# Operations of two tensors moved from GpSimd to VectorE, inverses built from blocks of 16, attention tiles spread anew

## The chip, the core and the metric

The kernel runs on one core of a Trainium2 chip. Its engines are TensorE (PE in the profile, with PEld for its weight loads), VectorE (DVE), ScalarE (ACT), GpSimd (POOL) and SyncE (SP), which issues nearly all DMAs. The metric is the device time of one execution in microseconds, as the median of several runs; lower is better.

## The reference, cut to what matters

The reference is two layers in fp32 on a sequence of 1024 positions and a width of 1024. Layer 0 mixes by an RWKV-7 recurrence (8 heads of 64) and by differential attention (4 heads); layer 1 mixes by a gated MLP over chunks of 128 positions. After each mixing comes a layer norm, a feed-forward block with a causal convolution of width 3, and another layer norm.

```
p   = x @ ab_w_in                                    # projections of both mixers
y_r = rwkv7_mix(p[..., :1792], ...)                  # state = state*w + (state@a) b^T + v k^T, per position
y_d = diff_attention(p[..., 1792:], ...)             # softmax(q1 k1) - lam * softmax(q2 k2), causal, then rms norm
x   = layer_norm(ALPHA*x + concat(y_r, y_d) @ ab_w_out)
ffn = (silu(conv3(x @ w_gate)) * (x @ w_val)) @ w_down   # width 2816
x   = layer_norm(ALPHA*x + ffn)
# layer 1: chunked_spatial_gating(x) @ c_w_out instead of the two mixers, then the same feed-forward
```

## The kernel before

Activations lie transposed: a tile is 128 features by 512 positions (half h of the sequence). Each dense product is done to nearly fp32 accuracy from fp32r operands: `split` makes `hi = copy(src)` on ACT and `lo = src - hi` on an engine with two-tensor operations, and `mm3` runs three 128x512 matmuls (lo·hi, hi·lo, hi·hi). So every weight and activation tile costs one ACT copy and one subtraction of two tensors ("a split" below). `split` (L125 to L128) does the subtraction on GpSimd unless an engine is given.

The program has five parts in time:

1. **Projections and RWKV, 0 to some 745 us.** The recurrence is cut into 8 units, four pairs of heads for each half of the sequence. A unit computes its vectors and masked 64x64 products, then inverts a unit triangular 64x64 matrix for each of its two heads and eight chunks, then runs a chain of small matmuls. The inverse takes 32x32 diagonal blocks: they are stored to DRAM and loaded so that one block lies on one partition (`N`, L938); 31 steps of forward substitution follow, each a multiplication and an addition on VectorE that need each other's result (L943, L945); the results go through DRAM again (`d<-X`, `D<-d`), four 32x32 transposes place them (L960, L967), and 16 and 16 small matmuls (L963, L972) make the lower left block. `weave` puts a slice of other work after every step of a chain: matmuls of later projections or of the output projection, and tiles of attention (a head is eight query tiles). A chain has 16 steps. The table `AT = 0, 0, 0, 9, 9, 9, 8, 0` says how many attention tiles are spread over the chain of each unit.
2. **Output projection and first layer norm**, to some 805 us.
3. **Feed-forward of layer 0**, to some 1430 us, as products of 2x2 blocks with sums of blocks (Strassen's form), so that sums (L312, L341) are formed on VectorE and split before PE uses them. First come 22 products with `A12`, then four early products with `A11`, then the loop over 22 feature tiles f: six products each, sums, convolution (L325, L327), gating, and stores of the gated tiles to DRAM. The splits of weights and of two of the four activation sums (`T2`, `T3`) are on GpSimd, as is one of the two gating multiplications (L332). In the down half of the block all splits are on VectorE already.
4. **Gated MLP of layer 1**, to some 1800 us; its weights' splits are on GpSimd (`B.weng`).
5. **Feed-forward of layer 1 and the last layer norm**, to the end.

The order on each engine is made by a list scheduler from priorities and a timeline of its own; PE instructions of the fill are pinned behind the last matmul of a chain step. Each engine executes its list in order.

Of the kernel before, what the change touches and what calls it, by code (L numbers as in the profile page):

```python
# [24 lines left out]
F32 = mybir.dt.float32  # L25
# [34 lines left out]
class Builder:  # L60
# [3 lines left out]
    def __init__(self, tc, ctx, a):  # L64
# [9 lines left out]
        self.onesD = c.tile([P, P], F32, name="onesD")  # L74
        nc.gpsimd.memset(self.onesD, 1.0 / D)
# [4 lines left out]
        self.weng = self.gs = None  # L80
# [44 lines left out]
    def split(self, src, hi, lo, eng=None):  # L125
        nc = self.nc
        nc.scalar.copy(hi, src)  # L127
        (eng or nc.gpsimd).tensor_tensor(out=lo, in0=src, in1=hi.bitcast(F32), op=ALU.subtract)  # L128

    def load_w(self, src, n=1024, extra=False):  # L130
# [11 lines left out]
        self.split(raw[:, :n], hi[:, :n], lo[:, :n], self.weng)  # L142
# [47 lines left out]
    def ln_stats(self, s, z):  # L190
# [9 lines left out]
        for d in range(KT):  # L200
# [26 lines left out]
    def ln_apply(self, s, z, rs, g, b, xhl, out):  # L227
# [3 lines left out]
        for d in range(KT):  # L231
# [23 lines left out]
    def ffn(self, layer, xa, xd, lng, lnb, out=None, xout=None):  # L255
# [32 lines left out]
        def operand(src, tiles, eng=None):  # L288
            hl = [tiles.pop(0) for _ in range(2)]
            self.split(src, *hl, eng)  # L290
# [6 lines left out]
        def load_up(f, todo):  # L297
# [8 lines left out]
            for n in todo:  # L306
# [6 lines left out]
                W[f][n] = operand(src, wt, vec if n in WLO and len(todo) < 5 else pool)  # L313
                yield

        def load_p2(f):
            raw = raws()[:, :HW]
            sync.dma_start(raw, wup[f][:, HW:])
            W[f]["A12"] = operand(raw, wt, pool)
# [11 lines left out]
        def store(f, h, c, v, eng=vec):  # L331
            eng.tensor_tensor(out=c, in0=c, in1=v, op=ALU.mult)  # L332
# [5 lines left out]
        def second(n, k, tiles):  # L338
# [3 lines left out]
            X[n].append(operand(o, tiles, vec if n in LOV else pool))  # L342
# [41 lines left out]
        for f in list(fs) + [None]:  # L384
# [10 lines left out]
            if old:  # L395
# [3 lines left out]
                store(g, 1, c1_, V_, pool)  # L399
# [47 lines left out]
        def make(n, i):  # L447
# [268 lines left out]
class Rwkv:  # L716
# [13 lines left out]
    def consts(self):  # L730
# [6 lines left out]
        self.mask = B.cload("cmask", [P, 3, C], pool=pool)  # L737
        self.rst = B.cload("rst", [P, P], a["rst"].broadcast_to([P, P]), pool=pool)
# [45 lines left out]
    def unit(self, h, p, xs, out):  # L784
# [141 lines left out]
        d1 = B.dram.tile([2, 2, NC, 32, 32], F32, name=B.uid("d1"))  # L926
        d2 = B.dram.tile([2, 2, NC, 32, 32], F32, name=B.uid("d2"))
# [341 lines left out]
AO = 0  # L1269
# [276 lines left out]
```

## Time and profile before

| | us |
|---|---|
| median of 3 runs | 2465.79 (2461.41 to 2466.0) |
| profiled execution | 2462.04 |
| its span | 2459.9 |
| PE busy, weight loads busy | 2339.2, 1887.6 |
| DVE, ACT, POOL busy | 1811.1, 1042.4, 875.2 |

The profiled execution's own time is its span and 2.1 us around it. "Busy" of PE counts each matmul from its start to its modelled end, and matmuls overlap in the pipe, so PE can be shown busy throughout and still have slack between short groups. Averages over the span say little here, because the parts above have different limits; the windows below are cut along the parts.

### The profile page before, as it was taken

How to read it: one execution, taken by the hardware profiler on the slowest of the kernel's cores; microseconds unless marked ns; L12 is line 12 of the kernel's file. 1: busy time of each engine (PE TensorE's matmuls, PEld its weight loads, DVE VectorE, ACT ScalarE, POOL GpSimd, SP SyncE). 2: the span in 40 equal slices, each digit the busy share in tenths (PEclk: the TensorE clock that was granted, in tenths of full speed). 3: DMA queues.
4: the chain of work that ended last, by engine and by line, in shares of the span. 5: the costliest groups of instructions: out<-in, count | busy, mean ns of one | idle time of the engine just before them, and what ended most of it. 6: DMA issues, size and time to landing. Idle time of an engine off the chain costs nothing. (4 is left out here: it accounts for less than half of the span.)

```text
span 2459.9 us, 34226 instructions
## 1 busy us (share of the span) xinstructions
PE 2339.2 (95%) x12058; PEld 1887.6 (77%) x12058; DVE 1811.1 (74%) x3308; ACT 1042.4 (42%) x1903; POOL 875.2 (36%) x770
## 2 busy tenths in 40 slices
PE   8999998888998989999999999999989999999996
PEld 6777777766776867888878878888877788887886
DVE  5766778899888757777689867345377777779875
ACT  4323455555554633333344435334353333334434
POOL 2001110110005756665600026557566666640003
PEclk9999998998999989999999999999999999999998
DMA  5322352332423644333485625234373333358441
GB/s 189 90 73 80 90 179 76 94 102 86 124 68 122 219 137 134 122 118 120 129 271 173 198 81 174 85 109 133 109 234 116 124 122 110 120 168 294 132 147 69
DMA packets 180508, 326.99 MB, mean 133 GB/s; under 512 B 44912, under 2 KB 58096, under 8 KB 180336
## 3 DMA queue, kind: packets, MB, share of 16 engines
q1 hardware_dynamic: 176112, 316.93, 40.5%
q10 hardware_dynamic: 4224, 7.87, 1.1%
q8 instruction: 95, 1.56, 0.3%
q14 instruction: 77, 0.63, 0.1%
HBM read 261.55 MB, written 63.18 MB: 132 GB/s over the span
## 5 line engine op out<-in xcount | busy, mean ns | idle before, releaser
L128 POOL TENSOR_TENSOR wlo<-wraw,whi 128x1024 fp32r<-128x1024 f32 x54 | 133.9, 2482 | 275.9 <-PE ch L150 168.1
L127 ACT CAST whi<-wraw 128x1024 fp32r<-128x1024 f32 (+1 forms) x166 | 153.8, 929 | 169.1 <-PE sc L150 45.8
L327 DVE SCALAR_TENSOR_TENSOR lx<-pr,cw,lx 128x512 f32<-128x512 f32 x176 | 182.6, 1038 | 4.2
L328 ACT ACTIVATE lx<-lx 128x512 f32<-128x512 f32 x88 | 55.7, 633 | 278.8 <-DVE lx L327 278.8
L148 PE MATMUL pj<-x,wlo 128*128 128x512 f32 x310 | 126.7, 409 | 9.8 <-DVE wlo L128 8.5
L149 PE MATMUL pj<-x,whi 128*128 128x512 f32 x303 | 121.6, 401 | 0.0
L150 PE MATMUL pj<-x,whi 128*128 128x512 f32 x303 | 120.7, 398 | 0.0
L325 DVE TENSOR_SCALAR lx<-pr,cw 128x512 f32<-128x512 f32 x88 | 78.5, 893 | 49.4 <-DMA gd<-lx 47.9
L332 POOL TENSOR_TENSOR lx<-lx,bv 128x512 f32<-128x512 f32 x44 | 69.5, 1579 | 78.4 <-ACT lx L328 73.9
L128 DVE TENSOR_TENSOR wlo<-wraw,whi 128x1024 fp32r<-128x1024 f32 x66 | 80.5, 1220 | 16.6 <-ACT whi L127 16.2
L148 PEld LDWEIGHTS pj<-x,wlo 128*128 128x128 f32 x310 | 59.7, 193 | 26.7 <-ACT x L127 7.3
L754 POOL COPY lastc<-pr 128x1 f32<-128x1 f32 x28 | 9.4, 334 | 187.2 <-ACT pr L752 187.2
L943 DVE TENSOR_TENSOR sub<-X,N 128x60 f32<-128x60 f32 (+24 forms) x248 | 51.6, 208 | 24.2 <-DMA N<-d 19.9
L202 POOL TENSOR_TENSOR sg<-sg,x 128x512 f32<-128x512 f32 x1 | 1.3, 1288 | 191.0 <-ACT x L199 191.0
L149 PEld LDWEIGHTS pj<-x,whi 128*128 128x128 f32 x303 | 58.5, 193 | 13.2 <-issue 1.4
L150 PEld LDWEIGHTS pj<-x,whi 128*128 128x128 f32 x303 | 58.2, 192 | 12.9 <-issue 0.4
L1224 ACT ACTIVATE ap<-ap,mx 128x128 f32<-128x128 f32 (+7 forms) x64 | 49.5, 773 | 43.1 <-DVE mx L1221 42.5
L1216 PE MATMUL sc<-x,x 128*128 128x512 f32 (+2 forms) x192 | 58.1, 407 | 7.8 <-DVE mx L1221 4.5
L128 POOL TENSOR_TENSOR whi<-wraw,whi 128x512 fp32r<-128x512 f32 x32 | 46.7, 1460 | 26.2 <-ACT whi L127 23.5
L128 POOL TENSOR_TENSOR wlo<-wraw,wlo 128x512 fp32r<-128x512 f32 x32 | 46.1, 1439 | 27.2 <-ACT wlo L127 27.0
L945 DVE TENSOR_TENSOR X<-X,sub 128x60 f32<-128x60 f32 (+24 forms) x248 | 51.6, 208 | 4.9
L148 PE MATMUL pq<-x,wlo 128*128 128x512 f32 x128 | 52.6, 411 | 2.7 <-DVE wlo L128 2.7
(1755 smaller groups left out, 8079.6 us busy)
## 6 DMA issues: line engine op xcount, KB each, us to landing
wraw<-in_w_up_dram SPq DMA_DIRECT2D x64, 512.0 KB, 4.1
wraw<-in_w_dq_dram SPq DMA_DIRECT2D x104, 256.0 KB, 3.5
gd<-lx SPq DMA_DIRECT2D x88, 256.0 KB, 2.3
KB<-in_w_up_dram SPq DMA_DIRECT2D x32, 512.0 KB, 3.5
wraw<-in_w_rwkv_dram SPq DMA_DIRECT2D x28, 512.0 KB, 3.7
KB<-in_w_dq_dram SPq DMA_DIRECT2D x50, 256.0 KB, 3.3
lx<-gd SPq DMA_DIRECT2D x48, 256.0 KB, 3.6
pr<-ge SPq DMA_DIRECT2D x44, 256.0 KB, 2.7
```

The source lines that it names most:

```text
L127: nc.scalar.copy(hi, src)
L128: (eng or nc.gpsimd).tensor_tensor(out=lo, in0=src, in1=hi.bitcast(F32), op=ALU.subtract)
L148: mm(ps, wl, xh, start=first, stop=False, **kw)
L149: mm(ps, wh, xl, start=False, stop=False, **kw)
L150: self.last = mm(ps, wh, xh, start=False, stop=last, **kw).ins
L325: vec.tensor_scalar(out=c, in0=G[:, 0:HW], scalar1=cw[:, f, 0:1], scalar2=cw[:, f, 3:4], op0=ALU.mult, op1=ALU.add)
L327: vec.scalar_tensor_tensor(out=c, in0=G[:, j:j + HW], scalar=cw[:, f, j:j + 1], in1=c, op0=ALU.mult, op1=ALU.add)
L328: act.activation(c, c, AF.Silu)
L332: eng.tensor_tensor(out=c, in0=c, in1=v, op=ALU.mult)
L943: dve.tensor_tensor(out=t, in0=X[:, 0:n, j:j + 1].broadcast_to([P, n, w]), in1=N[:, j:j + 1, j + 1:].broadcast_to([P, n, w]), op=ALU.mult)
L945: self.sub = dve.tensor_tensor(out=X[:, 0:n, j + 1:], in0=X[:, 0:n, j + 1:], in1=t, op=ALU.add)
L1216: nc.tensor.matmul(ps[:, :max(w, 256)], q, k[c][s][:, :max(w, 256)], start=i == 0, stop=i == 1)
```

## The change

1. `split`, `load_w`, `operand`, `store`, `ln_stats` and `ln_apply` lose their choice of engine: the subtraction of every split, the second sum of squares of a norm and both gating multiplications are VectorE operations. On GpSimd stay the subtraction and the scaling of three of eight tiles in the last norm (`PD`), four shifts, one masking product, the powers of small tiles (`rsqrt`), copies and memsets. GpSimd's list shrinks from 742 rows to 274.
2. The inverse starts from 16x16 diagonal blocks: 15 steps of substitution on a tile that holds 2 blocks in a partition's rows, with operands of 8 to 36 elements, where 31 steps had 16 to 76. Two levels of joining follow on PE in 32x32 tiles of the array: 32 matmuls (L968), a masked multiplication (L973), 32 and 16 matmuls (L974, L981), four additions into `XF` and two into `D0`, then 16 and 16 matmuls as before (L987, L994). The stores and loads through DRAM are 8, 2, 2 and 8 DMAs where there were 4, 4, 4 and 4.
3. A chain has 18 steps, `weave` divides by 18, and `AT` gives 10, 10, 10, 5 attention tiles to units 4 to 7.
4. `onesD` is one column, read with a stride of zero.

```diff
-    def split(self, src, hi, lo, eng=None):
+    def split(self, src, hi, lo):
         nc.scalar.copy(hi, src)
-        (eng or nc.gpsimd).tensor_tensor(out=lo, in0=src, in1=hi.bitcast(F32), op=ALU.subtract)
+        nc.vector.tensor_tensor(out=lo, in0=src, in1=hi.bitcast(F32), op=ALU.subtract)
...
-                (nc.vector if d in LNV else nc.gpsimd).tensor_tensor(out=hl[1], in0=z[d], in1=hl[0].bitcast(F32), op=ALU.subtract)
+                nc.vector.tensor_tensor(out=hl[1], in0=z[d], in1=hl[0].bitcast(F32), op=ALU.subtract)
...
-                W[f][n] = operand(src, wt, vec if n in WLO and len(todo) < 5 else pool)
+                W[f][n] = operand(src, wt)
...
-            X[n].append(operand(o, tiles, vec if n in LOV else pool))
+            X[n].append(operand(o, tiles))
...
-                store(g, 1, c1_, V_, pool)
+                store(g, 1, c1_, V_)
...
+        Q = 16
+        d1 = B.dram.tile([2, 4, NC, Q, Q], F32, name=B.uid("d1"))
+        d2 = B.dram.tile([2, 4, NC, Q, Q], F32, name=B.uid("d2"))
         for e in range(2):
-            for b in range(2):
-                rows = slice(64 * e + 32 * b, 64 * e + 32 * b + 32)
-                self.dq.dma_start(d1[e, b].rearrange("c s t -> s c t"), MA[rows, e, :, 32 * b:32 * b + 32])
-        I = 4 * NC
+            for b in range(4):
+                self.dq.dma_start(d1[e, b].rearrange("c s t -> s c t"),
+                                  MA[64 * e + Q * b:64 * e + Q * b + Q, e, :, Q * b:Q * b + Q])
+        I = 8 * NC
...
-        for j in range(31):
-            w, n = 31 - j, j // 4 + 1
+        for j in range(Q - 1):
+            w, n = Q - 1 - j, j // 2 + 1
...
+        dve.transpose(out=DT.rearrange("p c t -> p (c t)"), in_=D0.rearrange("p c t -> p (c t)"))
+        for c in range(NC):
+            for i, o in enumerate(R4):
+                B.last = nc.tensor.matmul(p1[o, 0, c], MA[o, i // 2, c, 32 * (i % 2):32 * (i % 2) + 32], DT[o, c], start=True,
+                                          stop=True, tile_position=(32 * i, 32 * i)).ins
+        yield
+        dve.tensor_tensor(out=T1, in0=p1[:, 0], in1=self.low[:, None, :].broadcast_to([P, NC, 32]), op=ALU.mult)
+        for c in range(NC):
+            for i, o in enumerate(R4):
+                B.last = nc.tensor.matmul(p1[o, 1, c], D0[o, c], T1[o, c], start=True, stop=True, tile_position=(32 * i, 32 * i)).ins
+        yield
         for lo, hi in H:
-            dve.transpose(out=XF[lo, :, 0:32], in_=D0[lo])
+            dve.tensor_tensor(out=XF[lo, :, 0:32], in0=p1[lo, 1], in1=DT[lo], op=ALU.add)
+        p0, p1 = p1, self.ps.tile([P, 2, NC, 32], F32, tag="ch", bufs=NBANK["ch"], name=B.uid("p1"))
+        for c in range(NC):
+            for i, o in ((1, R4[1]), (3, R4[3])):
+                B.last = nc.tensor.matmul(p1[o, 1, c], T1[o, c], D0[o, c], start=True, stop=True, tile_position=(32 * i, 32 * i)).ins
+        for lo, hi in H:
+            dve.tensor_tensor(out=XF[hi, :, 32:64], in0=p0[hi, 1], in1=DT[hi], op=ALU.add)
+            dve.tensor_tensor(out=D0[hi], in0=p1[hi, 1], in1=D0[hi], op=ALU.add)
...
-AT = 0, 0, 0, 9, 9, 9, 8, 0
+AT = 0, 0, 0, 10, 10, 10, 5, 0
...
-            for _ in range((j * na + AO) // 16 - ((j - 1) * na + AO) // 16):
+            for _ in range((j * na + AO) // 18 - ((j - 1) * na + AO) // 18):
...
-        weave(i, fill, (FC, max(total / 16, FR[i] if i < 6 else 0)), AT[i])
+        weave(i, fill, (FC, max(total / 18, FR[i] if i < 6 else 0)), AT[i])
```

**VectorE, the substitution of the last unit.** `X_6600` before and `X_6902` now are the tile of the unit's inverse; ap, mx, f are of the attention, y, bv, BK of other units. Before:

```order
L945 TENSOR_TENSOR X_6600<-X_6600,sub_6616 128x29
L1227 RECIPROCAL f_6422<-l_6393 128x1
L1051 TENSOR_TENSOR y_6514<-y_6514,bv_4644 128x512
L1221 ISA ap_6408,mx_6417<-sc_6414,zero,mx_6412 128x384
L1221 ISA mx_6417 128x1
L943 TENSOR_TENSOR sub_6619<-X_6600,N_6599 128x28
L1052 TENSOR_TENSOR y_6514<-y_6514,pl_6521 128x512
L886 TENSOR_TENSOR bv_6530<-v_5873,bs_6528 128x512
L990 COPY BK_5084<-pf_6820 64x512
L1221 ISA ap_6408,mx_6419<-sc_6414,amask,mx_6417 128x128
L1221 ISA mx_6419 128x1
L945 TENSOR_TENSOR X_6600<-X_6600,sub_6619 128x28
```

Now:

```order
L947 TENSOR_TENSOR sub_6910<-X_6902,N_6901 128x15
L1072 TENSOR_SCALAR y_6812<-y_6812,c_rvec 128x512
L949 TENSOR_TENSOR X_6902<-X_6902,sub_6910 128x15
L1073 TENSOR_TENSOR y_6812<-y_6812,bv_4792 128x512
L947 TENSOR_TENSOR sub_6913<-X_6902,N_6901 128x14
L1074 TENSOR_TENSOR y_6812<-y_6812,pl_6819 128x512
L949 TENSOR_TENSOR X_6902<-X_6902,sub_6913 128x14
L1243 ISA ap_5798,mx_5802<-sc_5799,zero 128x128
L1243 ISA mx_5802 128x1
L947 TENSOR_TENSOR sub_6916<-X_6902,N_6901 128x26
```

The 62 instructions of a unit's substitution, one after the other and each in need of the one before, are 30 with half the elements. Here they stood over 157 rows of VectorE's list, between attention and other units' work, and stand over 46.

**TensorE, where the chain of the last unit begins.** `p` is the bank in which the blocks are joined, av, sc, tr and ot are attention, wo is the output projection. Before, with the second group of 16 standing 27 rows after the first:

```order
L150 MATMUL wo_7196<-x_5838,whi_7192 128x512
L148 MATMUL wo_7286<-x_5808,wlo_7283 128x512
L1240 MATMUL av_7065<-x_5565,x_5568 128x128 x4
L963 MATMUL p_7547<-XT_7544,MB_5931 32x32 x16
L1216 MATMUL sc_7221<-x_5564,x_5556 128x256
L1216 MATMUL sc_7221<-x_5560,x_5556 128x256
```

Now, the first of four places:

```order
L148 MATMUL wo_7527<-x_6000,whi_7523 128x512
L1258 MATMUL tr_6464<-ident,ap_6439 128x128 x2
L1262 MATMUL av_6468<-x_5709,x_5712 128x128 x2
L968 MATMUL p_7788<-XN_7786,MB_6124 32x32 x32
L1262 MATMUL av_6468<-x_5709,x_5712 128x128 x2
L1262 MATMUL av_6468<-x_5710,x_5711 128x128 x2
L1238 MATMUL sc_6565<-x_5707,x_5700 128x512
```

and the last two of them, which answer to the two groups of before:

```order
L1238 MATMUL sc_6584<-x_5702,x_5698 128x512
L148 MATMUL wo_7619<-x_6012,whi_7615 128x512
L780 MATMUL pl_7733<-lx_2483,lw_7731 128x512
L987 MATMUL p_7890<-XT_7785,MB_6124 32x32 x16
L1262 MATMUL av_6535<-x_5709,x_5711 128x128 x4
L1262 MATMUL av_6535<-x_5710,x_5712 128x128 x3
L994 MATMUL p_7890<-T_7787,D_6908 32x32 x16
L1005 MATMUL pf_7964<-LT_6125,XT_7785 64x128
```

Between these stand the 48 of L974 and L981, alternating, 19 rows after the group of 32; each group of the chain waits for a VectorE or ScalarE result of the one before.

**VectorE, where the loop of the first feed-forward block begins.** Lines L341 (now L339) form the activation sums, L250 and L128 (now L248 and L126) are splits, L312 (now L310) forms weight sums, L394 (now L392) adds a product to the gate. Before:

```order
L341 TENSOR_TENSOR k_6714<-k_6714,aa_6710 128x512
L341 TENSOR_TENSOR BK_7543<-BK_7543,LT_7541 128x512
L250 TENSOR_TENSOR x_8230<-BK_7543,x_8229 128x512
L341 TENSOR_TENSOR BK_7543<-BK_7543,LT_7541 128x512
L128 TENSOR_TENSOR x_8216<-e_6712,x_8215 128x512
L128 TENSOR_TENSOR x_8218<-e_6713,x_8217 128x512
L128 TENSOR_TENSOR x_8220<-k_6714,x_8219 128x512
L312 TENSOR_TENSOR sg_6709<-wraw_8348 128x512
L312 TENSOR_TENSOR k_6714<-KB_8350,wraw_8348 128x512
L312 TENSOR_TENSOR e_6713<-sg_6709,KB_8350 128x512
L312 TENSOR_TENSOR aa_6710<-KB_8350,e_6713 128x512
```

Now:

```order
L339 TENSOR_TENSOR BK_7784<-BK_7784,LT_7782 128x512
L126 TENSOR_TENSOR Z_8670<-aa_6960,Z_8670 128x512
L126 TENSOR_TENSOR x_8548<-e_6963,x_8547 128x512
L339 TENSOR_TENSOR BK_7784<-BK_7784,LT_7782 128x512
L126 TENSOR_TENSOR Y_8673<-MB_7783,XT_8672 128x512
L126 TENSOR_TENSOR x_8550<-k_6964,x_8549 128x512
L392 TENSOR_TENSOR pr_6968<-pr_6968,pj_8255 128x512
L126 TENSOR_TENSOR dg_8675<-BK_7784,Y_8674 128x512
L310 TENSOR_TENSOR sg_6959<-wraw_8678 128x512
L126 TENSOR_TENSOR o_8677<-BK_7784,y_8676 128x512
L126 TENSOR_TENSOR wlo_8656<-wraw_8678,wlo_8656 128x512
L310 TENSOR_TENSOR k_6964<-KB_8680,wraw_8678 128x512
```

The splits that had a list of their own on GpSimd now stand in VectorE's list between the sums, and what waits there for a load or a PE result holds them up as well.

## Rows read from the trace of the kernel before

**Rows 1.** The page's head: span, and busy time of each engine.

```profile
span 2459.9 us, 34226 instructions
...
PE 2339.2 (95%) x12058; PEld 1887.6 (77%) x12058; DVE 1811.1 (74%) x3308; ACT 1042.4 (42%) x1903; POOL 875.2 (36%) x770
```

**Rows 2.** Busy time by stretch: stretch, length, engines' busy us, PE's granted clock, DMA.

```profile
60.00:380.00 320.00, 316.35 (x2161) 249.62 (x2160) 228.87 (x554) 122.64 (x213) 33.25 (x74) 0.98 0.36 105
380.00:740.00 360.00, 322.60 (x2441) 258.24 (x2441) 318.95 (x1042) 203.94 (x480) 32.91 (x60) 0.91 0.31 89
...
860.00:960.00 100.00, 87.17 (x349) 68.29 (x348) 63.56 (x74) 35.12 (x63) 57.45 (x50) 0.93 0.41 133
960.00:1200.00 240.00, 239.01 (x1032) 193.31 (x1031) 180.77 (x205) 81.71 (x145) 150.55 (x129) 1.00 0.38 123
1280.00:1400.00 120.00, 120.00 (x525) 98.75 (x524) 107.11 (x176) 55.15 (x96) 0.00 (x0) 0.99 0.61 201
1500.00:1780.00 280.00, 280.00 (x1296) 231.57 (x1295) 132.86 (x228) 106.61 (x151) 165.48 (x91) 1.00 0.35 113
...
1840.00:1950.00 110.00, 97.51 (x394) 75.73 (x393) 81.86 (x91) 35.79 (x64) 67.24 (x56) 0.95 0.38 124
```

**Rows 3.** The page's costliest groups: tiles and shapes, count, busy us, mean ns, idle before.

```profile
L128 POOL TENSOR_TENSOR wlo<-wraw,whi 128x1024 fp32r<-128x1024 f32 x54 | 133.9, 2482 | 275.9 <-PE ch L150 168.1
...
L128 DVE TENSOR_TENSOR wlo<-wraw,whi 128x1024 fp32r<-128x1024 f32 x66 | 80.5, 1220 | 16.6 <-ACT whi L127 16.2
...
L943 DVE TENSOR_TENSOR sub<-X,N 128x60 f32<-128x60 f32 (+24 forms) x248 | 51.6, 208 | 24.2 <-DMA N<-d 19.9
...
L945 DVE TENSOR_TENSOR X<-X,sub 128x60 f32<-128x60 f32 (+24 forms) x248 | 51.6, 208 | 4.9
```

**Rows 4.** VectorE's groups with shapes kept apart, whole span.

```profile
L943 DVE TENSOR_TENSOR sub<-X,N 128x60 f32<-128x60 f32 x24 | 5.2, 217 | 0.4
...
L943 DVE TENSOR_TENSOR sub<-X,N 128x28 f32<-128x28 f32 x16 | 3.0, 185 | 0.3
...
L877 DVE TENSOR_TENSOR MB<-pm,c_cmask 128x256 f32<-128x256 f32 x32 | 13.4, 419 | 13.6 <-PE pm L875 13.5
...
L960 DVE STREAM_TRANSPOSE XT<-D 32x256 f32<-32x256 f32 x16 | 6.9, 433 | 7.9 <-DMA D<-d 7.7
```

**Rows 5.** PE in order of time, last unit's first small group: start, us, records.

```profile
685.58 1.09 PE L963 MATMUL p<-XT,MB 32*32 32x32 f32 x32
```

**Rows 6.** The same view at 168 us: 64x64 matmuls on two tiles in turn.

```profile
168.65 1.01 PE L902 MATMUL pw<-Z,MB 64*64 64x64 f32 x27
```

**Rows 7.** GpSimd in order of time, before the first and the second feed-forward loop.

```profile
842.97 1.63 POOL L128 TENSOR_TENSOR Z<-MB,Z 128x512 fp32r<-128x512 f32 x1 [1.89 <-ACT Z L127]
...
856.50 1.74 POOL L128 TENSOR_TENSOR dg<-BK,Y 128x512 fp32r<-128x512 f32 x1
...
1810.16 1.75 POOL L250 TENSOR_TENSOR x<-MB,x 128x512 fp32r<-128x512 f32 x1
...
1832.33 1.73 POOL L128 TENSOR_TENSOR o<-BK,y 128x512 fp32r<-128x512 f32 x1
```

**Rows 8.** VectorE in order of time, before the second feed-forward loop.

```profile
1806.57 0.68 DVE L128 TENSOR_TENSOR MB<-sg,MB 128x512 fp32r<-128x512 f32 x1
1807.17 0.68 DVE L341 TENSOR_TENSOR cs<-cs,r 128x512 f32<-128x512 f32 x1
...
1815.80 1.79 DVE L341 TENSOR_TENSOR e<-e,sg 128x512 f32<-128x512 f32 x1
```

**Rows 9.** What PE waited for from 860 to 960 us: total, times, longest.

```profile
PE ch L148 <- ACT bv L403: 5.2, 1, 5.2
PE pj L148 <- DVE pr L394: 3.4, 1, 3.4
```

**Rows 10.** VectorE's groups in the first feed-forward loop, 960 to 1200 us.

```profile
L327 DVE SCALAR_TENSOR_TENSOR lx<-pr,cw,lx 128x512 f32<-128x512 f32 x58 | 65.6, 1131 | 1.5
L325 DVE TENSOR_SCALAR lx<-pr,cw 128x512 f32<-128x512 f32 x30 | 27.9, 929 | 12.2 <-DMA gd<-lx 11.6
```

**Rows 11.** Waits of the whole span, the one of the convolution.

```profile
DVE lx L325 <- DMA gd<-lx: 47.9, 24, 4.8
```

More of the change, by code (lines that the diff above doesn't have):

```diff
@@ L73, in __init__ @@
         c = self.const
-        self.onesD = c.tile([P, P], F32, name="onesD")
-        nc.gpsimd.memset(self.onesD, 1.0 / D)
+        ones = c.tile([P, 1], F32, name="onesD")
+        nc.gpsimd.memset(ones, 1.0 / D)
+        self.onesD = ones.broadcast_to([P, P])
         self.ident = c.tile([P, P], F32, name="ident")
@@ L286, in ffn, with operand @@
         ra, rbc = Ring(self.ln.tiles), Ring(self.up.tiles)
-        def operand(src, tiles, eng=None):
+        def operand(src, tiles):
             hl = [tiles.pop(0) for _ in range(2)]
-            self.split(src, *hl, eng)
+            self.split(src, *hl)
             return hl
@@ L737, in consts @@
         self.mask = B.cload("cmask", [P, 3, C], pool=pool)
+        self.low = B.cload("low", [P, 32], pool=pool)
         self.rst = B.cload("rst", [P, P], a["rst"].broadcast_to([P, P]), pool=pool)
@@ L945, in unit @@
             self.sub = dve.tensor_tensor(out=X[:, 0:n, j + 1:], in0=X[:, 0:n, j + 1:], in1=t, op=ALU.add)
-        for g in range(4):
-            self.dq.dma_start(d2.rearrange("e b c (m g) t -> g (e b c) m t", g=4)[g], X[I * g:I * g + I])
+        for g in range(2):
+            self.dq.dma_start(d2.rearrange("e b c (m g) t -> g (e b c) m t", g=2)[g], X[I * g:I * g + I])
         yield True
         XF = self.t("XT", 1, (P, NC, C))
-        D0 = self.t("D0", 1, (P, NC, 32))
-        T1 = self.t("XN", 1, (P, NC, 32))
+        DT = self.t("XN", 1, (P, NC, 32))
@@ L961, in unit @@
-        for e, (lo, hi) in enumerate(H):
-            for c in range(NC):
+            for b in range(4):
+                self.dq.dma_start(D0[64 * e + Q * b:64 * e + Q * b + Q, :, b % 2 * Q:b % 2 * Q + Q],
+                                  d2[e, b].rearrange("c s t -> s c t"))
+        dve.transpose(out=DT.rearrange("p c t -> p (c t)"), in_=D0.rearrange("p c t -> p (c t)"))
[3 more added lines that the diff above has]
+                                          stop=True, tile_position=(32 * i, 32 * i)).ins
@@ L963, in unit @@
+        for c in range(NC):
[4 more added lines that the diff above has]
+            dve.tensor_tensor(out=D0[hi], in0=p1[hi, 1], in1=D0[hi], op=ALU.add)
+        for c in range(NC):
+            for e, (lo, hi) in enumerate(H):
                 B.last = nc.tensor.matmul(p1[hi, 0, c], MA[lo, e, c, 32:64], XF[lo, c, 0:32], start=True, stop=True,
@@ L966, in unit @@
         for lo, hi in H:
-            dve.transpose(out=XF[hi, :, 32:64], in_=D0[hi])
-        for lo, hi in H:
             act.copy(T1[hi], p1[hi, 0])
-        for e, (lo, hi) in enumerate(H):
-            for c in range(NC):
+        for c in range(NC):
+            for e, (lo, hi) in enumerate(H):
                 B.last = nc.tensor.matmul(p1[hi, 1, c], D0[hi, c], T1[hi, c], start=True, stop=True,
@@ L1515, in layout @@
     a["cmask"] = np.stack([strict, incl, strict], 1)
+    a["low"] = (s[:, None] % 32 >= 16) & (np.arange(32) < 16)
     a["rst"] = (np.arange(128) % 64 != 0).astype(f32)[None]
```

45 lines of the change are left out of this document (20 added, 25 removed).

## The prediction

> **What bounds the kernel now.** I first read the page's head and the busy time by engine: PE is busy 2339 of 2460 us [rows 1], so at most 121 us are open to any change that leaves the matmuls as they are. Then the windows by stretch, to see where these 121 us lie [rows 2]. The projections with the first units (60 to 380) leave 3.7 us of 320, the first feed-forward loop (960 to 1200) 1.0 of 240, the gated MLP (1500 to 1780) none. Two kinds of stretch leave much: the units with attention (380 to 740), 37.4 us of 360, and the entries of the two feed-forward loops, 12.8 of 100 and 12.5 of 110. Next the groups of the page and VectorE's groups by form, for the price of one instruction [rows 3, 4], and the engines in order of time at the places where the change acts [rows 5 to 8]; last the waits, for what PE lacks at a loop's entry [rows 9] and what VectorE lacks in the loop [rows 10, 11].
>
> The profiled execution took 2462.0 us, 2.1 of them outside its span, and 3.8 less than the median of the runs. The sum is made against 2462.0; since the profiled time lies low in a spread of 4.6 us, I add half of the 3.8 at the end. This kernel's measurement can't tell a difference under 0.2%, 4.9 us.
>
> **Term 1, substitution in units 5 to 8.** In 380 to 740 VectorE is busy 319 of 360 us, 89%, and PE idles 37 at a clock of 0.91: VectorE bounds here. A unit's substitution now is 31 steps of two instructions at 208 ns [rows 3], 62 x 0.208 = 12.9 us (L943 and L945 alike). Afterwards 15 steps of two, with a mean of some 25 elements. The forms give 185 ns at 28 elements and 217 at 60 [rows 4], 1 ns an element, so 182 ns: 30 x 0.182 = 5.5 us, 7.4 less. Of four transposes at 433 ns one stays: 1.3 less. New are seven VectorE operations (the masked product L973, four additions into XF, two into D0); the nearest row, a 256-wide one that reads PSUM, takes 419 ns [rows 4]: 2.9 more. Net 5.8 us a unit, 23 for four units. If PE follows VectorE fully, the stretch shrinks by 23/0.89 = 26; if the length is set by the chain's hops between engines, by nothing; all of PE's idle time is 37. I take 20, since the list of VectorE holds fewer rows between a chain's ends (46 where 157 stood) and VectorE was the fuller engine, but not fully busy. The attention is 35 tiles as before, and where they stand is within this term's range: with 10, 10, 10, 5 the last chain keeps five tiles beside it, where PE had filler from the output projection anyway.
>
> **Term 2, the joining on PE in units 1 to 4.** Small matmuls of a unit rise from 32 to 112 in the program's words, which are 64 and 224 records, since 32 records stand in half of a group. In 60 to 380 PE is full, so each costs. A group of 32 records on 32x32 tiles took 1.09 us [rows 5], 0.032 us each with the last one's tail of some 0.1 off; 27 of 64x64 on two tiles took 1.01 [rows 6], some 0.030 each with a last one's length of about 0.2 off. Before: 64 x 0.032 = 2.0 us. After: the 128 records of L968, L974 and L981 that go round all four row groups of the array I price at half, 0.016, as two pairs can run side by side; the other 96 at 0.030: 2.0 + 2.9 = 4.9 us, 2.9 more a unit. Bounds: all at 0.016 gives 1.5 more, all at 0.032 gives 5.1. For four units 12 us, 6 to 20. Units 5 to 8 pay the same 12 inside PE's idle 37 us: nothing; if term 1 took all of that idle time they would show too, which is why term 1 stands at 20 and not 37.
>
> The Trainium skill, "TensorEngine Tiling (Array Packing)", section "Instruction Overhead", gives every matmul an overhead of about 60 cycles, however narrow it is; by an estimate from it the 160 further records of a unit cost 25 ns each at full clock, 16 us for four units, and the sum would be 4 us higher. It lies close to the row's 0.030 and speaks against the half price above, though a group that rotates over four row groups is not in this trace.
>
> **Term 3, the entries of the two loops.** There the trace shows VectorE and GpSimd in lockstep. VectorE operations on 128x512 that meet no GpSimd work start 0.60 us apart and take 0.68; beside GpSimd's they take 1.79 [rows 8], as long as GpSimd's own, 1.75. GpSimd's 14 operations from 1810.16 to 1832.33 start 22.17 / 13 = 1.70 us apart [rows 7], and VectorE's with them. So a pair (one here, one there) costs 1.70, and two on VectorE alone 2 x 0.60 = 1.20. Before the second loop that gives 14 x 0.5 = 7 us. Before the first, 9 such operations stand from 842.97 to 856.50: 4.5. The first weight operands have five splits, which would go from some 1.3 to 0.6 each; counted half, since sums stand between them, 3.5 for both loops. Together 15. PE's waits there are for ScalarE and VectorE results, 5.2 and 3.4 us [rows 9], which both hang on these sums and splits. Bounds: 0, if the loads or ScalarE's copies are what is late, and 25, all that PE idles at the entries.
>
> **Terms at nothing, with their cover.** Loops in their steady part: in 240 us 129 GpSimd operations go to VectorE at 0.60, 77 us onto 181. What came from the lockstep goes: L327 has 58 at 1131 ns and L325 30 at 929 [rows 10]; at 0.60 they give back 31 and 10. So at most 217 of 240 us, less as the weight sums that met GpSimd also shorten. PE waits for nothing there, and VectorE stays below PE: 0. The cover is the 23 us or more that are left, and operands made ahead; the second rival is the case where it is gone. Gated MLP: 54 splits of 2.48 us on GpSimd become 1.22 on VectorE [rows 3], 66 us, and the other 37 operations 22, on 133: 221 of 280, under a PE that never waits: 0. The down halves have no GpSimd work already (1280 to 1400), so nothing changes. First layer norm, 780 to 800: its second sum of squares and splits leave GpSimd, 2 us less, an estimate between 0 and 4 from the same 0.5 per pair. The broadcast column, and 20 DMA issues a unit on SyncE where there were 16: no wait of PE rests on either, 0.
>
> **Sum.** 2462.0 - 20 + 12 - 15 - 2 = 2437, and half of 3.8 on it: 2439 us. The terms' bounds reach further than they are likely to go together; as the likeliest case's own range I take 2425 to 2455.
>
> **Rivals.**
>
> *The chain doesn't shorten.* A unit's chain now passes two more joins, each a PE group, an evacuation and a further group, and 8 DMAs where 4 stood before the substitution; VectorE's loads of N already cost 19.9 us of waits [rows 3]. If these hops take back what the 32 fewer instructions give, term 1 is 0: 2439 + 20 = 2459. For it: PE idles 37 us at 89% of VectorE, so it isn't VectorE alone. Against: weave puts filler between steps, and 18 steps hold as much as 16.
>
> *Matmuls quicken without GpSimd.* In the loop a 128x512 product takes 240/1032 = 232.6 ns, where GpSimd is idle (1280 to 1400) 120/525 = 228.6. If that is GpSimd's reading, two loops of 22 x 72 matmuls gain 3168 x 0.004 = 12.7 us, and with the small matmuls at their low price of 6 the time is 2439 - 13 - 6 = 2420. Against: in the gated MLP, where GpSimd is busiest (165 of 280), 280/1296 = 216 ns, though with narrower ones among them.
>
> *Slower: VectorE's one list.* In the loop the convolution's first operation waits for a buffer that a store has to leave (gd<-lx): 47.9 us in 24 waits [rows 11], 11.6 in these 240 us [rows 10]. Until now the weight splits ran on meanwhile in GpSimd's list; now they stand behind that wait. If half of it reaches PE, it costs 24 us, and the entries, where the same list decides, lose their 15: 2439 + 24 + 15 = 2478. With the entries' gain kept it decides from 23 us of PE idle in the loops upwards. For it: VectorE at up to 217 of 240 with waits of 12 a stretch is nearly full. Against: the wait is idle time that exists because VectorE was early, and a fuller VectorE comes later and finds the store done.
>
> **How the numbers follow.** The forecast 0.50, the quick matmuls 0.17, the unshortened chain 0.14, the one list 0.15, and 0.04 for nothing that counts. The range of 8 in 10 takes in the forecast, most of the quick matmuls, all of the unshortened chain and the low end of the slower case: 2408 to 2468. Faster by over 0.2% (under 2461): 0.49 of the forecast, 0.17, and 0.08 of the unshortened chain, 0.74. Within 0.2%: the rest of that chain's case 0.05, and 0.04 for the last, 0.09. Slower: 0.17, the one list with the tails.
>
> **What would show it.** Term 1: 30 substitution instructions a unit near 182 ns, and the stretch from 380 to the output projection some 20 us shorter at VectorE's share of about 89%; wrong, if PE's idle time there stays near 37. Term 2: four joins a unit with 64 records at about 1.0 us (L968) and PE in the first units some 3 us a unit longer; the low bound shows as 0.016 a record in all. Term 3: VectorE's 128x512 operations 0.60 apart at the entries, GpSimd near 100 us in all, and PE's idle time there 10 and 8 us smaller; wrong, if PE then waits for loads. Terms at nothing: PE idle in 240 us of a loop still 1 to 2 us; if it is over 8, the slower rival runs. The prediction is wrong as a whole if the loops' 72 matmuls a tile take other than 72 x 0.2326 = 16.7 us, since that alone is worth more than any term.

## The result and the profile after

The changed kernel took 2426.11 us in the median (2419.77 to 2431.42), the kernel before 2464.34 in the same session: a ratio of 0.9845, with a 95% interval of 0.9816 to 0.9874, or 38 us less. The forecast was 2439, its own range 2425 to 2455. The profiled execution took 2419.77 us. Its page begins:

```profile
span 2418.0 us, 36296 instructions
...
PE 2320.2 (96%) x13338; PEld 1887.3 (78%) x13338; DVE 1855.9 (77%) x3555; ACT 1053.3 (44%) x1903; POOL 146.3 (6%) x291
```

GpSimd fell from 875 to 146 us [rows 1], and TensorE has 1280 records more (8 units of 160). PE's busy time fell by 19 us in spite of them; the entries below show why. Busy time by stretch in the changed kernel, with the columns of [rows 2]:

```profile
60.00:380.00 320.00, 308.22 (x2667) 243.81 (x2665) 200.67 (x429) 116.92 (x201) 30.91 (x66) 0.98 0.34 95
380.00:740.00 360.00, 325.01 (x3133) 260.37 (x3134) 302.77 (x924) 204.42 (x482) 37.44 (x61) 0.91 0.29 81
860.00:960.00 100.00, 93.78 (x402) 76.28 (x401) 92.05 (x152) 50.49 (x88) 4.72 (x11) 0.97 0.54 179
960.00:1200.00 240.00, 240.00 (x1043) 195.58 (x1042) 194.70 (x308) 86.05 (x147) 8.39 (x30) 1.00 0.37 121
...
1500.00:1780.00 280.00, 280.00 (x1304) 232.33 (x1303) 178.37 (x307) 110.99 (x160) 6.91 (x10) 1.00 0.38 121
1840.00:1950.00 110.00, 110.00 (x479) 89.69 (x479) 92.74 (x149) 40.02 (x70) 4.20 (x14) 1.00 0.41 132
```

In 380 to 740 PE idles 35 us where it idled 37: the stretch that was to gain most is as it was, though VectorE's share fell from 89 to 84%. The first units idle 11.8 where they idled 3.7. The entry of the second loop idles 0 where it idled 12.5.

Fixed windows don't meet the same work in two kernels, so the gain was placed between events that both have: from the first activation sum of a feed-forward block (line L341 of before, L339 of after) to the first convolution of its fifth tile, and from there to that of its 21st. Before:

```profile
825.90:949.30 123.40, 111.19 (x455) 88.36 (x453) 88.85 (x96) 53.29 (x97) 76.14 (x60) 0.94 0.51 169
949.30:1217.60 268.30, 266.68 (x1149) 215.48 (x1150) 201.88 (x228) 91.98 (x164) 166.94 (x143) 1.00 0.38 120
1797.70:1914.40 116.70, 105.52 (x433) 83.34 (x431) 93.36 (x95) 51.16 (x92) 76.59 (x58) 0.96 0.53 170
1914.40:2182.40 268.00, 264.23 (x1137) 212.58 (x1136) 208.88 (x230) 91.44 (x163) 170.06 (x144) 1.00 0.37 119
```

The changed kernel, the same four:

```profile
852.90:945.40 92.50, 86.18 (x368) 69.77 (x367) 85.46 (x142) 50.18 (x87) 4.54 (x10) 0.96 0.55 186
945.40:1210.90 265.50, 265.50 (x1154) 216.39 (x1153) 215.00 (x341) 95.76 (x163) 9.09 (x32) 1.00 0.39 124
1783.60:1877.30 93.70, 93.70 (x410) 76.76 (x409) 86.31 (x144) 51.11 (x91) 2.51 (x9) 1.00 0.61 203
1877.30:2142.30 265.00, 265.00 (x1153) 216.21 (x1152) 214.83 (x340) 95.53 (x163) 9.26 (x33) 1.00 0.38 122
```

The sums of the first block begin 27.0 us later than before, those of the second 14.1 earlier, and the second entry alone is 23 us shorter. So what lies before the sums got slower, and the feed-forward's entries gave back more: 30.9 and 23.0 us between these events. ScalarE begins to normalize the attention's last tile at 745.7 us, 20 us later than before (725.8). Not all of the 27.0 is lost: part of the first block's opening products run in the meantime, and at the fifth tile's convolution the changed kernel leads by 3.9 us.

VectorE in order of time at the entry of the second block, changed kernel:

```profile
1818.24 0.69 DVE L126 TENSOR_TENSOR whi<-k,whi 128x512 fp32r<-128x512 f32 x1
1818.84 0.69 DVE L310 TENSOR_TENSOR aa<-KB,e 128x512 f32<-128x512 f32 x1
1819.44 0.69 DVE L126 TENSOR_TENSOR whi<-e,whi 128x512 fp32r<-128x512 f32 x1
1820.05 0.54 DVE L323 TENSOR_SCALAR lx<-pr,cw 128x512 f32<-128x512 f32 x1
```

Where each operation took 1.79 us beside GpSimd's [rows 8], they now start 0.60 us apart, splits and sums in one list.

### The profile page after: what moved, and what is told of

Its sections match the earlier page's. It is cut to its first block, busy times and chain, and to the rows that moved or that the text cites. A ratio compares the mean times of both kernels' runs of the same rounds, so it can differ in the third digit from the quotient of the medians.

```text
span 2418.0 us, 36296 instructions
## 1 busy us (share of the span) xinstructions
PE 2320.2 (96%) x13338; PEld 1887.3 (78%) x13338; DVE 1855.9 (77%) x3555; ACT 1053.3 (44%) x1903; POOL 146.3 (6%) x291
## 4 chain that ended last, share of the span: by engine, by line
PE 78%; DVE 10%; DMA 7%; ACT 2%; issue 2%; SPq 1%; POOL 0%; ACTq 0%; DVEq 0%; POOLq 0%
PE ch L146 6%; PE ch L148 6%; PE ch L147 6%; PE pj L146 6%; PE pj L148 6%; PE pj L147 6%; PE at L147 4%; PE at L146 4%; PE at L148 4%; PE sc L146 4%; PE sc L148 4%; PE sc L147 4%; PE pf L1005 2%; DVE x L126 1%; PE pm L874 1%
## 5 line engine op out<-in xcount | busy, mean ns | idle before, releaser
L126 DVE TENSOR_TENSOR wlo<-wraw,whi 128x1024 fp32r<-128x1024 f32 x120 | 146.4, 1221 | 69.7 <-ACT whi L125 66.6
L325 DVE SCALAR_TENSOR_TENSOR lx<-pr,cw,lx 128x512 f32<-128x512 f32 x176 | 131.4, 747 | 1.6
L1246 ACT ACTIVATE ap<-ap,mx 128x128 f32<-128x128 f32 (+7 forms) x64 | 49.6, 775 | 55.3 <-DVE mx L1243 54.7
L147 PE MATMUL pq<-x,whi 128*128 128x512 f32 x128 | 52.0, 407 | 0.0
L405 POOL COPY pr<-pr 128x2 f32<-128x2 f32 x44 | 21.6, 491 | 497.5 <-DVE pr L392 444.7
L148 PE MATMUL pq<-x,whi 128*128 128x512 f32 x128 | 51.5, 403 | 0.0
L148 PE MATMUL at<-x,whi 128*128 128x512 f32 x131 | 51.5, 393 | 0.0
L147 PE MATMUL at<-x,whi 128*128 128x512 f32 x131 | 51.1, 390 | 0.0
L323 DVE TENSOR_SCALAR lx<-pr,cw 128x512 f32<-128x512 f32 x88 | 47.7, 542 | 3.4 <-DMA gd<-lx 3.3
L125 ACT CAST x<-wraw 128x512 fp32r<-128x512 f32 x56 | 34.4, 618 | 34.1 <-DMA wraw<-in_w_dq_dram 16.0
L874 PE MATMUL pm<-LT,KB 64*128 64x128 f32 x256 | 40.0, 314 | 7.0 <-DVE KB L863 7.0
L1262 PE MATMUL av<-x,x 128*128 128x128 f32 x288 | 41.7, 285 | 3.9 <-ACT x L1259 3.6
```

The source lines that it names most:

```text
L126: nc.vector.tensor_tensor(out=lo, in0=src, in1=hi.bitcast(F32), op=ALU.subtract)
L147: mm(ps, wh, xl, start=False, stop=False, **kw)
L148: self.last = mm(ps, wh, xh, start=False, stop=last, **kw).ins
L323: vec.tensor_scalar(out=c, in0=G[:, 0:HW], scalar1=cw[:, f, 0:1], scalar2=cw[:, f, 3:4], op0=ALU.mult, op1=ALU.add)
L325: vec.scalar_tensor_tensor(out=c, in0=G[:, j:j + HW], scalar=cw[:, f, j:j + 1], in1=c, op0=ALU.mult, op1=ALU.add)
L874: nc.tensor.matmul(pm[:, i], KB[O[e], c0 + i], LAR[O[e], c0 + i], start=True, stop=True)
```

## The experiments

All ratios are against the kernel before, run in the same session, with 95% intervals. In one line each:

| kernel | ratio | interval |
|---|---|---|
| moves alone | 0.982 | 0.980 to 0.9841 |
| moves, new table | 0.9812 | 0.9792 to 0.9832 |
| inverse, steps and table alone | 1.0066 | 1.004 to 1.0092 |
| changed kernel, old table | 0.9884 | 0.9863 to 0.9905 |
| weight splits alone | 0.9842 | 0.982 to 0.9863 |
| T2, T3 splits alone | 0.9961 | 0.9944 to 0.9977 |
| moves, two more hops | 0.9864 | 0.9841 to 0.9886 |
| moves, joins doubled | 0.9893 | 0.987 to 0.9915 |
| moves, half the substitution | 0.9824 | 0.9801 to 0.9847 |
| changed kernel, wide joins | 0.9875 | 0.9852 to 0.9897 |
| moves, new table, heads in turn | 0.9783 | 0.9759 to 0.9806 |
| the last with 13 steps | 0.9774 | 0.9755 to 0.9793 |

**Taking the change apart.** Four kernels. The moves alone are the changed kernel with the whole inverse (its first lines stand for it), the step count and the table of before:

```diff
-        for j in range(Q - 1):
-            w, n = Q - 1 - j, j // 2 + 1
+        for j in range(31):
+            w, n = 31 - j, j // 4 + 1
...
-            for _ in range((j * na + AO) // 18 - ((j - 1) * na + AO) // 18):
+            for _ in range((j * na + AO) // 16 - ((j - 1) * na + AO) // 16):
-AT = 0, 0, 0, 10, 10, 10, 5, 0
+AT = 0, 0, 0, 9, 9, 9, 8, 0
```

> All operations of two tensors on VectorE as in the changed kernel, but the inverse from blocks of 32, 16 steps and the old attention table. Theory A, the terms of the prediction: 17 us under before (entries 15, layer norm 2), 2447. Theory B, from the two traces: from the first feed-forward block on the changed kernel is some 60 us faster and before it 20 us slower, so this version keeps the 60 alone: 2400 to 2412, faster than the changed kernel. A third: the gain needs both parts, since VectorE is relieved by the inverse and loaded by the moves; then the part before the feed-forward is slower here than in the changed kernel and the time is 2430 or more.

The inverse alone is the converse: before, with the new inverse, 18 steps, the new table and the one-column constant.

> The kernel before with the inverse from blocks of 16, 18 steps, the table 10, 10, 10, 5 and the one-column constant; GpSimd keeps its operations. Theory A: -20 + 12 = 8 us faster, 2456. Theory B: 10 to 20 us slower, 2474 to 2484, and the attention ends some 20 us later than in before.

Two more set only `AT`:

> The changed kernel with the old table 9, 9, 9, 8. Theory A: as the changed kernel within 5 us, 2421 to 2431. Theory B: the table is what lets the attention end 20 us later, at 746 us; then it ends near 725 here and the time is 10 to 20 us shorter, 2406 to 2416. A rival of B: the end of the attention comes from the 18 steps and the small matmuls, so it stays near 746 and the time at 2426.

> As the version with the moves alone (old inverse, 16 steps) but the table 10, 10, 10, 5. Theory A: equal to the version with the moves alone within 5 us. Theory B, if the table delays the attention: 10 to 20 us slower than that version; if the inverse delays it: equal.

Theory B was right in direction and nearly in size, against the prediction's terms; its times, 2400 to 2412 and 2474 to 2484, were missed by 1 and by 4 us. The moves give 44 us by themselves (2413.14 against 2456.92). The inverse with its steps costs 13 when alone (2469.64) and 11 on top of the moves (2424.33 against 2413.14, both with the old table; their ratios of 0.9884 and 0.982 have intervals apart, and by them it is 16). With the new table the ratios, 0.9845 and 0.9812, give 8, and their intervals overlap. So the cost lies between 8 and 16. Its claim on the table fell: the old one is no faster under the new inverse, and the new one no slower under the old. The moves alone, between the same events:

```profile
826.00:931.70 105.70, 105.70 (x463) 86.59 (x462) 89.59 (x146) 55.53 (x99) 1.58 (x9) 1.00 0.60 202
931.70:1198.00 266.30, 266.30 (x1157) 217.06 (x1156) 215.49 (x342) 95.43 (x163) 9.41 (x33) 1.00 0.36 120
1774.80:1868.90 94.10, 94.10 (x412) 77.02 (x411) 86.20 (x143) 50.99 (x91) 2.50 (x9) 1.00 0.60 202
1868.90:2134.20 265.30, 265.30 (x1153) 216.22 (x1152) 214.98 (x341) 95.56 (x163) 9.25 (x33) 1.00 0.36 121
```

The first sum starts at 826.0 us where it started at 825.9: nothing came from the norm before it. The first entry gives 17.7 us, the second 22.6, the two loops 2.0 and 2.7, what lies between loop and entry (down half, norm, gated MLP) 3.3, what follows the second loop 1.4: together 49.7, where the spans of 2459.9 and 2410.3 differ by 49.6. That is 6 more than the medians of one session give; the profiled execution of before is from another session, and the parts may be some us too large. The 3.3 can't be put down to the moves: the inverse alone, which leaves GpSimd its operations, takes 576.6 us for the same stretch where before takes 580.1 and the moves alone 576.8.

**Which operations at the entry.** In before, the engine of the weights' splits or of two of the four sums' splits, and nothing else:

```diff
-                W[f][n] = operand(src, wt, vec if n in WLO and len(todo) < 5 else pool)
+                W[f][n] = operand(src, wt, vec)
-            W[f]["A12"] = operand(raw, wt, pool)
+            W[f]["A12"] = operand(raw, wt, vec)
```

> The kernel before with only the splits of the weight operands of the two feed-forward loops on VectorE; the splits of T2 and T3, the gating, the norms and the gated MLP keep GpSimd. Theory B1: at a loop's entry VectorE is full and every operation that meets GpSimd's costs 0.85 us instead of 0.60; the weights are most of GpSimd's operations there (some 45 of 58 between 1798 and 1914 us), so most of the 46 us go: 28 to 40 us faster, ratio 0.984 to 0.989. Theory B2: what TensorE lacks at the entry are the splits of T2 and T3 that stand in GpSimd's list, so this gives 10 us or less, ratio over 0.995.

```diff
-LOV = "T1,T4"
+LOV = "T1,T2,T3,T4"
```

> The kernel before with only the splits of T2 and T3 on VectorE (8 operations in each of the two blocks). Theory B1: 16 operations at 0.25 to 0.5 us, 4 to 8 us faster, ratio 0.996 to 0.999. Theory B2: most of the moves' gain, 25 us or more, ratio under 0.990.

B1 held. The weights give 38 us (2422.95 against 2460.80), the sums 8. What VectorE and GpSimd do there together counts by number: in 116.7 us the two engines did 95 and 58 operations, 153, one each 0.76 us; the moves alone do 143 and 9 in 94.1 us, one each 0.62. An entry lasts to about the fifth tile, not only to the first weight operands. Two things change together here, and no run parts them: VectorE no longer meets GpSimd's operations, and each split is done sooner. In before, the 83 of GpSimd's 425 operations of two tensors on 128x512 that meet no VectorE operation take 1.29 us in the mean, where VectorE needs 0.68.

**Hops or matmuls.** The inverse's cost has two candidates: TensorE's time for more small matmuls, and more hops between engines in a unit's chain. The first kernel shortens the new groups:

```diff
-        for c in range(NC):
-            for i, o in enumerate(R4):
-                B.last = nc.tensor.matmul(p1[o, 1, c], D0[o, c], T1[o, c], start=True, stop=True, tile_position=(32 * i, 32 * i)).ins
+        for i, o in enumerate(R4):
+            B.last = nc.tensor.matmul(p1[o, 1], D0[o, 0], T1[o], start=True, stop=True, tile_position=(32 * i, 32 * i)).ins
```

> The changed kernel with the three new groups of small matmuls as 4, 4 and 2 matmuls of 256 columns with the stationary block of the first chunk, instead of 32, 32 and 16 of 32 columns: the other chunks' inverses are not those of the reference. Every hop of the chain stays, TensorE's own time for the groups falls from 2.9 to some 0.6 us a unit. If the inverse from blocks of 16 costs its 8 to 13 us by TensorE's time, 8 x 2.3 = 18 us go where TensorE is full: 10 to 18 us under the changed kernel, a ratio of 0.977 to 0.981. If it costs them by two more hops of the chain, nothing changes: 0.984 to 0.988.

It came out level with the changed kernel or above, but settles little. Added up over the records of all eight units, the small matmuls of the joins cover 29.3 us in the changed kernel and 26.3 here, so 3.0 us were taken away, not 18. The next two add one thing each to the moves alone, the first with 18 steps for its two further slices. A hop here is two matmuls and the two VectorE operations that need them, 0.42 us each. Hops, after the last join:

```diff
+        for k in range(2):
+            for e, (lo, hi) in enumerate(H):
+                B.last = nc.tensor.matmul(p1[lo, k, 0], XF[lo, 0, 0:32], XF[lo, 0, 0:32], start=True, stop=True,
+                                          tile_position=(64 * e, 64 * e)).ins
+            yield
+            for lo, hi in H:
+                dve.scalar_tensor_tensor(out=XF[lo, :, 0:32], in0=p1[lo, k, 0:1].broadcast_to([32, NC, 32]), scalar=0.0,
+                                         in1=XF[lo, :, 0:32], op0=ALU.mult, op1=ALU.add)
```

> The version with the moves alone (inverse from blocks of 32, old table) with two more hops at the end of the joining: two 32x32 matmuls, then two VectorE operations of 256 elements that need them, and 18 steps in a chain. TensorE's added work is some 0.1 us a unit, VectorE's 1.7. If hops are what the inverse from blocks of 16 costs, this version is 8 to 14 us slower than the moves alone, a ratio of 0.985 to 0.988; if TensorE's time for the small matmuls is, it stays within 4 us of it, 0.980 to 0.984.

Matmuls, in both joins:

```diff
-            for c in range(NC):
+            for c in [c for c in range(NC) for _ in range(2)]:
```

> The version with the moves alone, with each small matmul of the two joins issued twice: 64 records more a unit, some 2.1 us of TensorE, as much as the change added, with no further hop. By term 2 of the prediction units 1 to 4 pay it, 8 us: ratio 0.984 to 0.987; if all eight pay, 17 us and 0.988 to 0.991. If the small matmuls fall into time that TensorE has anyway: within 4 us of the moves alone, 0.980 to 0.984.

Both cost. Two hops a unit cost 11 us by the ratios (0.0044 of 2461; the intervals touch), within the 8 to 16 of the new inverse. In the trace, unit 6, the four records of a hop are followed by other work until VectorE is done (start, duration, engine, line):

```profile
543.07 1.73 PE L971 MATMUL p<-XN,D 32*32 32x32 f32 x32 [0.33 <-ACT XN L968]
...
546.62 0.32 PE L978 MATMUL p<-XT 32*32 32x32 f32 x4
...
551.20 0.25 PE L978 MATMUL p<-XT 32*32 32x32 f32 x4
...
554.91 0.74 PE L990 MATMUL pf<-LT,XT 64*64 64x128 f32 x3 [0.27 <-DVE XT L982]
```

From the second join to the first use of its result (L990) 11.8 us pass, where 2.6 passed in the moves alone (565.97 to 568.53). In each of the eight units the two hops lengthen this stretch, by 6 to 17 us. Doubled matmuls cost 18 us (0.0073). The joins' records cover 40.7 us there and 19.7 in the moves alone, 21 more over all eight units, so they cost about their own time. The doubled groups of unit 5:

```profile
489.50 1.91 PE L962 MATMUL p<-XT,MB 32*32 32x32 f32 x32 [1.32 <-DVE XT L959]
...
492.28 1.91 PE L962 MATMUL p<-XT,MB 32*32 32x32 f32 x32
...
497.72 3.43 PE L971 MATMUL p<-XN,D 32*32 32x32 f32 x64
```

The first stands at 489.5 us where the moves alone have it at 465. These groups are slow: 64 records took 2.11 us in 10 of the 16 groups, and here two halves took 1.91 each and the second group 3.43. From 488 to 502 us the granted clock was 0.50. From 400 to 500 us it was 0.84, and 0.95 in the moves alone. What lowered it there isn't shown.

As a clock of progress, the moved columns of all matmuls but the joins were added up in order of time. At 311 us, behind the joins of units 1 to 3, the doubled kernel is 8 us behind the moves alone, and its joins' records cover 7.6 more; the changed kernel is 3 behind and covers 3.4 more; the one with two hops is level at 337. So there, where PE is full, matmuls cost about their own time and hops nothing. At 1000 us, behind all units, the three are 26, 13 and 14 us behind, so in the later units both cost. The clock is good to some 5 us: the run of the next paragraph, with half the substitution and no further matmul, is 3 behind at 311 and 5 at 1000.

That leaves the cause of the new inverse's 8 to 16 us open. Its small matmuls cover 29.3 us where 19.7 stood, and these 9.6 us, at the price of the doubled ones, would be nearly all of it. Its further hops, at the price of the two added here, would be too. Together they would be more than was measured, and no run parts them.

**The substitution by itself.** In the moves alone:

```diff
-        for j in range(31):
+        for j in range(15):
```

> The version with the moves alone, with 15 of the 31 steps of substitution left out (the later columns of each block's inverse are missing): 32 VectorE instructions a unit less, the whole of what the blocks of 16 save there, with no further hop or matmul. By term 1 of the prediction VectorE bounds units 5 to 8, and 4 x 6.4 us go, up to 20 to 26: ratio 0.972 to 0.975. If the length of these units is set by the chain's hops and the substitution runs beside the chain of the unit before, it is within 6 us of the moves alone: 0.980 to 0.984.

No gain from 16 of the 31 steps left out: 0.9824 against 0.982. Busy time from 400 to 740 us, the moves alone:

```profile
400.00:740.00 340.00, 308.38 (x2370) 245.96 (x2369) 301.12 (x997) 198.18 (x466) 32.21 (x57) 0.92 0.32 90
```

and with half the substitution:

```profile
400.00:740.00 340.00, 305.42 (x2340) 243.22 (x2339) 278.96 (x867) 195.70 (x465) 36.43 (x57) 0.91 0.31 89
```

VectorE has 22 us less to do, and PE idles 34.6 us instead of 31.6. VectorE doesn't bound these units.

**A faster version.** The old inverse with the loops of the two joins exchanged, as the changed kernel has them in its last two groups:

```diff
-        for e, (lo, hi) in enumerate(H):
-            for c in range(NC):
+        for c in range(NC):
+            for e, (lo, hi) in enumerate(H):
...
```

> The version with the moves, the inverse from blocks of 32 and the table 10, 10, 10, 5, with the small matmuls of the two joins in the changed kernel's order (the two heads in turn, where the eight chunks of one head came first). The changed kernel's groups of 32 in that order take 0.7 us where 1.1 stood: 0.8 us a unit. If TensorE's time for them counts in all units, 6 us less than with the old order, a ratio of 0.978 to 0.980; if not, equal to it, 0.979 to 0.983. Either way the fastest version of those tried or level with it.

```profile
618.15 0.69 PE L962 MATMUL p<-XT,MB 32*32 32x32 f32 x32
619.68 0.69 PE L971 MATMUL p<-XN,D 32*32 32x32 f32 x32 [0.84 <-ACT XN L968]
```

Each group takes 0.69 us where it took 1.09 [rows 5]. The median of 2402.36 us is 7 below that of the same kernel with the old order (2409.32, an earlier session); the intervals overlap, so the 6 us expected are likely and not shown. It beats before by 2.2%, and its interval ends below the changed kernel's (0.9806, where that begins at 0.9816). With 13 steps, where the halves of three pairs of steps become one:

```diff
                 (act.copy, dve.tensor_copy)[e](BM[e][o, c0:c0 + 4], pf[o])
-            yield
+        yield
...
```

> The fastest version so far (moves, blocks of 32, the two heads in turn, 10, 10, 10, 5) with 13 steps in a chain instead of 16: three pairs of steps whose halves don't need each other become one step each, so the chain has the same links and the same matmuls and the fill is cut in 13 slices. If it is the number of slices that the two further steps of the inverse from blocks of 16 cost, this one gains 5 us or more, a ratio under 0.976; if it is the links, where TensorE has to wait for VectorE or ScalarE, nothing changes: 0.976 to 0.981.

Nothing changed (0.9774 against 0.9783): the number of slices isn't the cost. The run keeps every link and every matmul of the chain, so it doesn't choose between those two.

## Why the prediction was right, and where it was wrong

The total was right and the first three terms were not: the entries were too small by some 20 to 25 us, the other two summed to -8 where the runs give +8 to +16, and these errors of opposite sign cancelled in great part. That the time lay in the range, 1 us above its lower end, was luck to that extent.

**Term 3, the entries, -15, measured -40 in the two profiled executions.** By the medians all moves together gave 44, so the entries gave some 35 to 40. That the splits and sums at the entries are what PE lacked was right; the size was wrong in two steps. "Before the second loop that gives 14 x 0.5 = 7 us" counted the pairs to 1832 us; the lockstep goes on to the fifth tile, with 58 GpSimd operations from 1797.7 to 1914.4. And "25, all that PE idles at the entries" was no upper bound, because PE's busy time holds lost time too. In before, after a wait for VectorE at the second entry, PE in order of time:

```profile
1845.51 0.77 PE L148 MATMUL sc<-LT,whi 128*128 128x512 f32 x1 [4.25 <-DVE pr L394]
1846.08 0.63 PE L149 MATMUL sc<-LT,whi 128*128 128x512 f32 x1
1846.51 0.63 PE L150 MATMUL sc<-LT,whi 128*128 128x512 f32 x1
...
1851.62 0.39 PE L150 MATMUL pj<-LT,wlo 128*128 128x512 f32 x1
1851.85 0.39 PE L148 MATMUL pj<-LT,wlo 128*128 128x512 f32 x1
```

and the busy time by stretch just there:

```profile
1845.50:1851.40 5.90, 5.89 (x14) 4.64 (x15) 5.40 (x6) 2.53 (x4) 2.73 (x4) 0.50 0.48 167
```

After 4.25 us of idleness the matmuls start 0.43 us apart, at a granted clock of 0.50, the lower of the two levels (1.2 GHz), and only after 14 of them 0.23 apart. The window counts those 5.9 us as fully busy. In the two entries 41 matmuls ran so, 8.2 us beyond 0.227 each, and 25 longer gaps held 28.2 us more: 36.4 lost, where 25 had been set as the bound. In the moves alone both entries have neither, and the clock is 1.00. What else the second entry gave is some 20 matmuls that run in the loop behind it (433 records became 412, 1137 became 1153).

**Term 1, -20, measured nothing.** The step that failed is "VectorE bounds here", and its own sign of being wrong came: PE idles 35 us there. The prices held: an instruction of the substitution takes 173 to 188 ns against the 182 of the estimate, in the changed kernel's groups by shape:

```profile
L947 DVE TENSOR_TENSOR sub<-X,N 128x30 f32<-128x30 f32 x24 | 4.5, 188 | 0.5
...
L947 DVE TENSOR_TENSOR sub<-X,N 128x14 f32<-128x14 f32 x16 | 2.8, 173 | 0.4
```

But half the substitution left out is worth nothing: VectorE, busy 89% beside an idle PE, did not bound here. That both wait in the units' chains is the reading that is left, and it was not tested by itself. The first rival had this term at 0 too, by hops that "take back what the 32 fewer instructions give". But the run with half the substitution has no further hop, so there was nothing to take back; hops cost on top. The rival's time of 2459 did not come, because term 3 hid it.

**Term 2, +12.** Its size a unit and its place were wrong, its sum by chance near. The groups are cheaper than priced; unit 6 of the changed kernel:

```profile
509.51 0.75 PE L968 MATMUL p<-XN,MB 32*32 32x32 f32 x64
...
516.37 0.62 PE L974 MATMUL p<-T,D 32*32 32x32 f32 x48
...
521.47 0.69 PE L987 MATMUL p<-XT,MB 32*32 32x32 f32 x32 [1.85 <-DVE D L984]
...
523.00 0.84 PE L994 MATMUL p<-T,D 32*32 32x32 f32 x32 [0.84 <-ACT T L991]
```

64 records in 0.75 us are 0.012 us each, less than the low bound of 0.016, and the two-head groups 0.022 instead of 0.030. By their records the joins of units 1 to 4 cover 14.2 us where 9.6 stood in the moves alone, 1.1 more a unit and not 2.9. Units 5 to 8, which the prediction let pay "nothing", have 5.0 more, and the run with doubled matmuls shows that matmuls cost there too. From the first record above to the last group's end lie 14.3 us, with waits for VectorE and ScalarE in front of the last two; in the moves alone the joins of unit 6 stand within 9.5. The run with two more hops shows that such length costs as well. Which of the two made the 8 to 16 us stays open. The Trainium skill, "TensorEngine Tiling (Array Packing)", "Instruction Overhead", has some 60 cycles of overhead for every matmul; by an estimate 25 ns at full clock. A record measured here, where four row groups take turns, takes half of that; a matmul of the program, which is two records, takes 23 ns.

**Terms at nothing.** The loops' steady part gained 2 to 3 us each: with the moves alone 266.30 / 1157 = 230.2 ns a record where 266.68 / 1149 = 232.1 stood. Most of that is not the second rival (4.0 ns by GpSimd's silence). In before, 7 starts of the first loop and 12 of the second come more than 0.26 us after the one ahead, 2.4 and 5.3 us beyond 0.227 each; in the moves alone none does. The other starts are 231.5 ns apart in before and 230.4 in the moves alone. So the rival is there at a quarter of its size, 1.1 ns or some 2.5 us in two loops. The gated MLP, the down halves and the norm between show nothing clear of the runs' spread, and the 2 us of the first norm did not come. GpSimd's busy time was put at near 100 us and is 146.

**The slower rival** didn't come. The wait it rested on nearly vanished; all of VectorE's waits on that store in the changed kernel:

```profile
DVE lx L323 <- DMA gd<-lx: 3.3, 8, 1.0
```

47.9 us had stood there [rows 11]. As its "against" had it, a fuller VectorE comes later and finds the store done; PE idles 0 in 240 us of the loop.

## What to carry to other kernels

Take the room of a stretch from the starts of its matmuls, not from PE's busy time: a wait also slows what runs after it, and busy time counts that as work. A busy engine beside an idle PE is not the bound until a kernel with less of its work is faster; here 22 us less on VectorE were worth nothing, while two more hops a unit cost 11 and 21 us more of small matmuls in the chains cost 18. Where two engines slow each other on the same kind of operation, count the operations of both over the whole stretch in which one of them is late, and try the parts of a change singly: the moves alone, with the two heads in turn, beat the whole.

## What was not expected of the hardware

- In before, after idle stretches of 5.21 and 4.25 us at the entries, PE ran its next matmuls at half the clock: 11 records from 894.5 to 899.0 us and 14 from 1845.5 to 1851.4, at a granted clock of 0.50.
- The order of small matmuls on the array sets their price: 32 records of 32x32 took 1.09 us with one head's eight chunks behind each other, 0.69 with the two heads in turn, and 64 took 0.75 over four row groups.
